# Pair 2 of the `up` product in seven half products, weight sums and sums of squares on GpSimd, and longer runs of feature matmuls, in a hybrid decoder layer on one core

## The chip, the cores and the metric

The kernel runs on one core of one Trainium2 chip. The metric is the time of one execution on the device, in microseconds (us). Three runs of the kernel before took 682.83 us in the median, from 681.87 to 683.28.

## The reference

One decoder layer over 512 tokens and 1024 features, all in float32. Two mixers (pooling over four windows, and sparse attention with 8 heads in 2 groups) are merged by gates and projected. A gated convolutional MLP follows. What the change touches is the two norms and the MLP's first product:

```
h = rms_norm(x, mix_norm_g)                 # mean of squares over 1024 features
proj = h @ w_in
...
x = x + (gate_pool * y_pool + gate_nsa * y_nsa) @ w_out
h = rms_norm(x, ffn_norm_g)
gate_pre, val = split(h @ w_up, 2)          # w_up: 1024 x 5632
gate_c = causal_dwconv(gate_pre, conv_w, conv_b)
x = x + (silu(gate_c) * val) @ w_down       # w_down: 2816 x 1024
```

## The kernel before

Everything is kept transposed: features on the 128 partitions, the 512 tokens along a row. A float32 product is made of three matmuls in a reduced format (`fp32r`): each operand is split into a high part and a low part (the rest), and high x high, high x low and low x high are added up in PSUM (`mm3`, line 479). So each weight tile `wraw` that a DMA brings is split into `whi` (ScalarE copies it into the reduced format) and `wlo` (VectorE subtracts, or ScalarE copies the negative and a DMA from GpSimd's queue adds the raw tile to it).

**Stages.** First the query and key projection with the sum of squares of the input (`square_x`, line 578; the sum goes through a matmul with ones, `norm_rstd`, line 588). Then attention, whose matmuls form the stream `m`, beside the feature products (gates, pooling, compression inputs), whose matmuls form the stream `f`; both share TensorE. Then the projections `wno` and `wout`, with the second sum of squares (line 1189). Then `up`: 22 pairs of 128 x 1024 weight blocks, one of the gate half and one of the value half. Products with `wdn` are filled in between pairs 5 and 18. Last the output stage with `wdz` (`dz_fast`, line 1419) in four pairs.

**Plain and fast pairs.** A plain pair (`up_plain`, line 1235) is two `mm3` over 8 blocks: 2 x 8 x 3 = 48 matmuls of 512 columns. A fast pair (`up_fast`, line 1343) takes the 2 x 2 block product with seven half products in the manner of Strassen: 7 x 4 x 3 = 84 matmuls of 256 columns (`product`, line 1261, with weights called a11, a12, h1 to h5). It needs sums of the weights (`half_weights`, line 1312): four additions of 128 x 512 tiles, s3 = first + r1, r1 = r1 + r2, rg = rg + r1, and the other half of rg plus the first; then each sum is split, some by a DMA from GpSimd's queue (`parts`, line 1320). `PLAIN = (0,2)` says that pairs 0 and 2 are plain. The output stage uses the same `half_weights` with tiles of 384 columns.

**Order.** The program is first recorded as a list of operations and then ordered by a planner (`Plan.run`, line 228, and `Plan.emit`, line 379): it prices each operation (`price`, line 199), plays the five engines' queues forward, and writes each engine's instructions in the order that it found. Each engine works through its own queue strictly in that order. On TensorE the planner picks between the heads of the streams `m` and `f` (line 301), by which has got less far.

All instructions are issued at line 422, so that in the profile the tile names tell them apart: `sl`, `sh` are the low and high part of a weight sum, `s`, `r`, `wraw` the sums and their sources, `th`, `tl`, `gh`, `gl`, `gp` parts of the normed input, `acc` and `sq` the sum of squares and one square, `mm`, `tr`, `av`, `sc` PSUM banks.

Of the kernel before, what the change touches and what calls it, by code (L numbers as in the profile page):

```python
# [49 lines left out]
NCST = _o  # L50
PAGES = 54
RINGS = {"wraw": 3, "whi": 3, "wlo": 3}
PLAIN = (0,2)
DIRECT = (0,)
AT = (5, 9, 13, 17)
FILL = {f: (0, 0, 0, 0) for f in range(22)}
# [1 line left out]
FILL.update({18: (0, 1, 0, 0), 19: (0, 0, 0, 0), 20: (0, 0, 0, 0), 21: (0, 0, 0, 0)})  # L58
TRIES = 12
RESERVE = 3  # L60
CUTS = (1, 2)
MORE = 4
BASE = 5.0
# [3 lines left out]
LANDS = (0.8, 0.8, 1.2, 1.2, 2.0, 2.0)  # L67
TRIALS = ((0.5, RATE), (0.8, RATE), (1.4, RATE), (0.8, 0.9 * RATE))
AHEAD = 4


def _span(x):
# [12 lines left out]
def _cols(x):  # L85
    n = 1
    for _, c in list(x.ap)[1:]:
        n *= c
    return n
# [23 lines left out]
class Plan:  # L113
# [45 lines left out]
    def note(self, eng, method, a, kw):  # L159
        if self.open is None or self.open == "new":  # L160
            op = Op(len(self.ops), eng, self.stream)
            op.deps.update(o.i for o in self.after)
            self.ops.append(op)
            if self.open == "new":
                self.open = op
        else:
            op = self.open
            assert op.eng == eng
        outs = [a[0]] if a else []
        outs += [v for k, v in kw.items() if k in self.OUT and v is not None]  # L170
        ins = [v for v in a[1:] if hasattr(v, "tensor")]
        ins += [v for k, v in kw.items() if k not in self.OUT and hasattr(v, "tensor")]
        op.calls.append((method, a, kw))
        cost, tail, land = self.price(eng, method, outs, ins, a, kw)
        op.cost += cost
        op.port |= eng == "POOL" and method[:6] == "tensor" or eng == "DVE" and not any(
            x.tensor.name in self.psum for x in ins)
        op.tail = tail
        op.land += land
        if kw.get("accum_op") is not None:  # L180
            ins.append(outs[0])
        for x, w in [(x, False) for x in ins] + [(x, True) for x in outs]:
            n = x.tensor.name
            if n not in self.tag:
                continue
            r = (0, 999, 0, 1 << 30) if n in self.psum and n not in self.fine else _span(x)
            past = list(self.writes.get(n, ()))
            if w:
                past += self.reads.get(n, ())
            for o, q in past:  # L190
                if o is not op and r[0] < q[1] and q[0] < r[1] and r[2] < q[3] and q[2] < r[3]:
                    op.deps.add(o.i)
            (self.writes if w else self.reads).setdefault(n, []).append((op, r))
            if not self.users[n]:
                op.allocs.append(n)
            if op not in self.users[n][-1:]:
                self.users[n].append(op)

    def price(self, eng, method, outs, ins, a, kw):
        n = max(_cols(x) for x in outs + ins)  # L200
        if method == "dma_start":
            x = outs[0]
            size = x.ap[0][1] * _cols(x) * 4 if hasattr(x, "ap") else 0
            return (0.87 if eng == "POOL" else 0.45), 0.0, size * (2.0 if kw.get("accum_op") is not None else 1.0)
        if eng == "PE":
            n = _cols(a[2])
            return max(n / 2250.0 + (0.005 if n < 300 else 0.0), 0.109), 0.17, 0
        if eng == "ACT":
            c = 0.19 + n * 0.000835
            if any(_cols(x) == 1 for x in ins):  # L210
                c += 0.09
            if kw.get("accum_out") is not None:
                c += 0.19
            if a[2] in (AF.Sin,):
                c += 1.28
            return c, 0.0, 0
        if eng == "DVE":
            wide = [x for x in ins if _cols(x) > 1]
            if method == "tensor_tensor_reduce":
                return 0.24 + n * 0.00105, 0.0, 0  # L220
            if len(wide) > 1 or method == "tensor_reduce" or any(x.tensor.name in self.psum for x in wide):
                return 0.15 + n * (0.00105 if method != "scalar_tensor_tensor" else 0.00114), 0.0, 0
            return 0.2 + n * 0.00054, 0.0, 0
        if method == "memset":
            return 0.1 + n * 0.0008, 0.0, 0
        return 0.12 + n * 0.0023, 0.0, 0

    def run(self, key, reserve, land, rate=RATE, fixed=None):
        ops = self.ops
# [17 lines left out]
        at = dict.fromkeys(heads, 0)  # L247
        done = {"m": 0.0, "f": 0.0}
        total = {s: sum(o.cost for o in l if s == "f" or self.span[0] <= o.i <= self.span[1]) for s, l in heads.items()}
        order = []  # L250

        def finish(o):
            for n in o.tiles:
# [42 lines left out]
        def pick(e):  # L296
            if fixed:
                o = fixed[e][count[e]] if count[e] < len(fixed[e]) else None
                w = None if o is None or o.left else when(o)
                return None if w is None else (w, o)  # L300
            if e == "PE":
                best = None
                for s, l in heads.items():
                    if at[s] < len(l) and not l[at[s]].left:
                        w = when(l[at[s]])
                        if w is not None:
                            first = (done["m"] <= min(done["f"] + self.lead, 0.999)) == (s == "m")
                            w2 = max(w - 0.1, clock[e]) if first else w + 1e-6
                            if best is None or w2 < best[0]:
                                best = (w2, w, l[at[s]])  # L310
                return best and (best[1], best[2])
            c = [(when(o), o) for o in pool[e]]
            c = [x for x in c if x[0] is not None]
            if not c:
                return None
            m = min(x[0] for x in c)
            return min(((key[o.i], w, o.i, o) for w, o in c if w <= m + 0.12))[1::2]

        dirty = dict.fromkeys(engs, True)
        while len(order) < len(ops):  # L320
            best = None
            for e in engs:
                p = pick(e)
                if p and (best is None or p[0] < best[0]):
                    best = p
            if settle(best[0] if best else 1e17):
                continue
            if best is None:
                raise RuntimeError("no order found: %d of %d" % (len(order), len(ops)))
            w, o = best  # L330
            o.start = w
            clock[o.eng] = w + o.cost
            if o.port:
                port[:] = [w + o.cost, o.eng]
            o.fin = w + o.cost + o.tail
            if o.land:
                queue[o.eng].append([w + o.cost + 0.7, o.land / rate, o])
            count[o.eng] += 1
            if o.eng == "PE":
                at[o.stream] += 1  # L340
                if o.stream == "f" or self.span[0] <= o.i <= self.span[1]:
                    done[o.stream] += o.cost / total[o.stream]
            else:
                pool[o.eng].remove(o)
            for n in o.allocs:
                g = self.tag[n]
                f = free[g]
                past = min(f)
                f.remove(past)
                for u in self.users.get(past[1], ()):  # L350
                    u.hand.append(o)
                if g in nxt:
                    nxt[g] += 1
                if n in self.early:
                    line[0] += 1
            order.append(o)
            if not o.land:
                finish(o)
# [67 lines left out]
def hybrid_layer(ctx: ExitStack, tc: tile.TileContext, xT, xa, pos, par, cst, poolw, w1, wa, wb, wf,  # L426
# [3 lines left out]
    PE, ACT, DVE, POOL, SP = pl.engines  # L430
# [98 lines left out]
    acc = page("acc")  # L529
# [48 lines left out]
    def square_x(k):  # L578
        if k == 0:
            ACT.activation(acc, xr[k], AF.Square)  # L580
        else:
            sq = page("sq")
            ACT.activation(sq, xr[k], AF.Square)
            DVE.tensor_add(acc, acc, sq)

    rb = keep("rb", (P, T))

# [137 lines left out]
    for t in range(NT):  # L725
        x, y = qp[t], kp[t]
# [182 lines left out]
    x = keep("kcx", (64, 1, DH))  # L909
    DVE.tensor_scalar_mul(x[:, 0], pk[0:64, 0:64], 0.5)  # L910
    sq = keep("kcs", (64, DH))
# [209 lines left out]
    for c in range(4):  # L1121
        wh, wl = weights(wno[c].rearrange("p a k n -> p (a k n)"), 1024, "v")
        for f in (2 * c, 2 * c + 1):
            o = (f % 2) * 512
# [3 lines left out]
            m = page("tn")  # L1128
# [16 lines left out]
    acc = page("acc")  # L1145
# [28 lines left out]
    for f in (0, 4, 1, 5, 2, 6, 3, 7):  # L1174
# [14 lines left out]
        if f:  # L1189
            sq = page("sq")  # L1190
            ACT.activation(sq, x2[f], AF.Square)
            DVE.tensor_add(acc, acc, sq)
        else:
            ACT.activation(acc, x2[f], AF.Square)
        if f > 3:
# [116 lines left out]
    def half_weights(first, second, w, dma, gate):  # L1312
# [16 lines left out]
        a1 = tuple(ring(n, F32R)[:, :2 * w] for n in ("whi", "wlo"))  # L1329
        split(*a1, rg)  # L1330
        s3 = soon("s3")[:, :w]
        DVE.tensor_add(s3, rg[:, :w], r1)
        h5 = parts(r2, dma[0])
        DVE.tensor_add(r1, r1, r2)
        h3 = parts(s3, dma[1])
        DVE.tensor_add(rg[:, :w], rg[:, :w], r1)
        h1 = parts(r1, dma[2])
        h2 = parts(rg[:, :w], dma[3])
        DVE.tensor_add(rg[:, w:], rg[:, w:], rg[:, :w])
        h4 = parts(rg[:, w:], dma[4])  # L1340
        return tuple(q[:, :w] for q in a1), tuple(q[:, w:] for q in a1), h1, h2, h3, h4, h5

# [106 lines left out]

    pl.emit(TRIES, RESERVE)  # L1450

# [93 lines left out]
```

## Time and profile before

| what | value |
|---|---|
| median of 3 runs | 682.83 us |
| the profiled execution's own time | 682.61 us |
| its span (first to last instruction) | 680.8 us |
| TensorE (PE) busy | 675.8 us, 99% |
| VectorE (DVE) busy | 529.2 us, 78% |
| ScalarE (ACT) busy | 446.5 us, 66% |
| GpSimd (POOL) busy | 106.9 us, 16% |
| mean granted TensorE clock | 0.999 |

A matmul's busy time overlaps the next one's, so what a matmul costs is read from the starts of two neighbours, or from a piece of the chain of waits with its count. In the chain each row is: start, duration, engine and what it wrote, and how many. In the timeline each row is: start, busy time, engine, operation, out<-in, shape, count, and in brackets idle time before it with what ended it. In the table by stretches of time, each engine's busy time stands with its instruction count behind it. GpSimd's rows named DMA are the time in which it issues the transfer; its spans are rough.

### The profile page before, as it was taken

What the parts mean: (1) busy time and instruction counts of PE and PEld (TensorE: products, weight loads), DVE (VectorE), ACT (ScalarE), POOL (GpSimd) and SP (SyncE); (2) the same over time, 40 slices, a digit from 0 to 9 for tenths busy, and PEclk for the clock granted to TensorE, in tenths of its full rate; (3) what the DMA queues carried; (4) which work ended last, traced back from release to release, by engine and by line L of the source; (5) the groups of instructions that cost most, each with busy time, mean ns of one, the idle gap of its engine ahead of it and who ended that gap; (6) DMA issues with size and microseconds to landing.
All of it is one profiled execution on the core that took longest, in us unless ns stands there. A gap on an engine that the chain in (4) does not pass through costs nothing.

```text
span 680.8 us, 11617 instructions
## 1 busy us (share of the span) xinstructions
PE 675.8 (99%) x4186; PEld 605.1 (89%) x4186; DVE 529.2 (78%) x1149; ACT 446.5 (66%) x821; POOL 106.9 (16%) x135
## 2 busy tenths in 40 slices
PE   9999999999999999999999999999999999999997
PEld 8898888888888888888898999999999999999897
DVE  6869777888877743868868988877777877888985
ACT  7677487777677653346777766667667665677552
POOL 0010111111100110001222222232212222222131
PEclk9999999999999999999999999999999999999999
DMA  8469656445455567845877778778859766775365
GB/s 303 146 160 273 156 133 161 109 125 143 120 143 136 127 150 245 286 152 171 232 167 194 167 164 189 187 172 197 188 127 191 199 156 168 177 164 129 70 145 154
DMA packets 49449, 115.34 MB, mean 169 GB/s; under 512 B 5616, under 2 KB 11632, under 8 KB 49392
## 3 DMA queue, kind: packets, MB, share of 16 engines
q1 hardware_dynamic: 31392, 76.44, 35.2%
q0 software_dynamic: 17856, 38.02, 31.2%
q8 instruction: 33, 0.54, 0.3%
q14 instruction: 24, 0.20, 0.1%
q10 hardware_dynamic: 144, 0.14, 0.1%
HBM read 70.28 MB, written 6.29 MB: 112 GB/s over the span
## 4 chain that ended last, share of the span: by engine, by line
PE 95%; DMA 2%; DVE 1%; ACT 0%; issue 0%; POOL 0%; SPq 0%; POOLq 0%; ACTq 0%
PE mm L422 37%; PE tr L422 33%; PE sc L422 14%; PE av L422 11%; DMA xr<-xT 1%; DMA sl<-wraw 1%; DMA r<-wdz 0%; DVE qp L422 0%; DVE small L422 0%; POOL sl L422 0%; SPq L422 0%; DVE vv L422 0%; ACT whi L422 0%; ACT xh L422 0%; ACT sl L422 0%
## 5 line engine op out<-in xcount | busy, mean ns | idle before, releaser
L422 ACT ACTIVATE whi<-wraw 128x1024 fp32r<-128x1024 f32 (+2 forms) x90 | 91.8, 1021 | 38.8 <-PE mm L422 13.2
L422 DVE TENSOR_TENSOR wlo<-wraw,whi 128x1024 fp32r<-128x1024 f32 (+1 forms) x62 | 72.4, 1169 | 4.6 <-ACT whi L422 4.2
L422 PE MATMUL mm<-xh,whi 128*128 128x512 f32 x176 | 71.3, 405 | 0.0
L422 PE MATMUL tr<-tl,sh 128*128 128x256 f32 x250 | 70.1, 280 | 0.0
L422 PE MATMUL mm<-xh,wlo 128*128 128x512 f32 x176 | 68.9, 391 | 0.0
L422 PE MATMUL mm<-xl,whi 128*128 128x512 f32 x176 | 68.7, 390 | 0.0
L422 PE MATMUL tr<-th,sl 128*128 128x256 f32 x240 | 67.7, 282 | 0.0
L422 PE MATMUL tr<-th,sh 128*128 128x256 f32 x240 | 67.7, 282 | 0.0
L422 POOL DMA_DIRECT2D wlo<-wraw x28 | 24.5, 877 | 240.3 <-ACT wlo L422 182.5
L422 POOL DMA_DIRECT2D sl<-r x44 | 38.0, 863 | 125.4 <-ACT sl L422 78.7
L422 PEld LDWEIGHTS tr<-tl,sh 128*128 128x128 f32 x250 | 47.2, 189 | 0.5
L422 PEld LDWEIGHTS tr<-th,sh 128*128 128x128 f32 x240 | 45.1, 188 | 1.1
L422 PEld LDWEIGHTS tr<-th,sl 128*128 128x128 f32 x240 | 45.1, 188 | 0.0
L422 ACT ACTIVATE u<-tr 128x256 f32<-128x256 f32 x40 | 15.4, 384 | 42.8 <-PE tr L422 42.3
L422 DVE SCALAR_TENSOR_TENSOR ft<-fg,pr,ft 128x511 f32<-128x511 f32 (+1 forms) x44 | 32.9, 748 | 12.0 <-ACT ft L422 11.5
L422 PE MATMUL sc<-yh,whi 128*128 128x512 f32 x108 | 42.2, 390 | 0.0
L422 PE MATMUL sc<-yl,whi 128*128 128x512 f32 x108 | 42.0, 389 | 0.0
L422 PE MATMUL sc<-yh,wlo 128*128 128x512 f32 x108 | 42.0, 389 | 0.0
L422 ACT ACTIVATE wlo<-wraw 128x1024 fp32r<-128x1024 f32 x28 | 29.7, 1061 | 16.0 <-PE mm L422 13.1
L422 PEld LDWEIGHTS mm<-xh,wlo 128*128 128x128 f32 x176 | 33.0, 188 | 7.3
L422 PEld LDWEIGHTS mm<-xh,whi 128*128 128x128 f32 x176 | 33.1, 188 | 5.6
L422 PEld LDWEIGHTS mm<-xl,whi 128*128 128x128 f32 x176 | 33.2, 188 | 5.5
(427 smaller groups left out, 2055.0 us busy)
## 6 DMA issues: line engine op xcount, KB each, us to landing
wlo<-wraw POOLq DMA_DIRECT2D x28, 512.0 KB, 4.7
wraw<-wup SPq DMA_DIRECT2D x24, 512.0 KB, 4.3
wraw<-wf SPq DMA_DIRECT2D x22, 512.0 KB, 3.6
r<-wup SPq DMA_DIRECT2D x40, 256.0 KB, 5.2
sl<-r POOLq DMA_DIRECT2D x40, 256.0 KB, 4.4
wraw<-wdn SPq DMA_DIRECT2D x16, 512.0 KB, 4.3
sl<-wraw POOLq DMA_DIRECT2D x20, 256.0 KB, 3.5
wraw<-wout SPq DMA_DIRECT2D x8, 512.0 KB, 3.6
```

The lines of the kernel that those rows point to most:

```text
L422: getattr(self.real[o.eng], method)(*a, **kw)
```

## The change

Four things change.

1. `PLAIN` loses pair 2, which so becomes a fast pair.
2. In `half_weights` two of the four additions (s3, and the last one into the second half of rg) move from VectorE to GpSimd, in the 21 fast pairs of `up` and the four of the output stage.
3. The 14 additions into `acc` of the two norms move from VectorE to GpSimd.
4. The planner keeps on with the stream `f` on TensorE, once it has begun it, until twelve matmuls in a row are placed, and prices GpSimd's two-input additions at 0.33 + 0.004 a column. It no longer marks operations that share a port; since nothing but DMAs and fills stood on GpSimd before, that mark had no effect there.

```
-PLAIN = (0,2)
+PLAIN = (0,)
...
+POOL2 = 0.004
...
+RUN = 12
...
-        op.port |= eng == "POOL" and method[:6] == "tensor" or eng == "DVE" and not any(
-            x.tensor.name in self.psum for x in ins)
...
-        return 0.12 + n * 0.0023, 0.0, 0
+        return 0.33 + n * (0.0026 if sum(_cols(x) > 1 for x in ins) < 2 else POOL2), 0.0, 0
...
                             first = (done["m"] <= min(done["f"] + self.lead, 0.999)) == (s == "m")
+                            if s == "f" and 0 < length[0] < RUN:
+                                first = True
+                            elif s == "m" and 0 < length[0] < RUN:
+                                first = False
...
+                length[0] = length[0] + len(o.calls) if o.stream == "f" else 0
...
             ACT.activation(sq, xr[k], AF.Square)
-            DVE.tensor_add(acc, acc, sq)
+            POOL.tensor_add(acc, acc, sq)
...
             ACT.activation(sq, x2[f], AF.Square)
-            DVE.tensor_add(acc, acc, sq)
+            POOL.tensor_add(acc, acc, sq)
...
         s3 = soon("s3")[:, :w]
-        DVE.tensor_add(s3, rg[:, :w], r1)
+        POOL.tensor_add(s3, rg[:, :w], r1)
...
-        DVE.tensor_add(rg[:, w:], rg[:, w:], rg[:, :w])
+        POOL.tensor_add(rg[:, w:], rg[:, w:], rg[:, :w])
         h4 = parts(rg[:, w:], dma[4])
```

What the planner makes of it is shown at three places. The first is GpSimd's queue while the second norm's squares are added up and the first fast pair's weights are made (`acc` is the sum of squares, `tl` and `gp` are parts of the normed input, `s`, `r` and `wraw` are weight sums). Before:

```order
L422 DMA tl<-tb 128x512
L422 DMA gp<-gh 128x256 x2
L422 DMA sl<-r_869 128x512
L422 DMA sl<-r_868 128x512
L422 DMA wlo<-wraw 128x1024
L422 DMA tl<-tb 128x512
L422 DMA wlo<-wraw 128x1024
L422 DMA sl<-wraw 128x512
```

And now:

```order
L427 DMA gp<-gh 128x256
L427 TENSOR_TENSOR acc<-acc,sq 128x512
L427 DMA gp<-gh 128x256
L427 DMA sl<-r_868 128x512
L427 DMA sl<-r_869 128x512
L427 TENSOR_TENSOR acc<-acc,sq 128x512
L427 DMA tl<-tb 128x512
L427 TENSOR_TENSOR wraw<-wraw 128x512
L427 DMA sl<-wraw 128x512
```

The last addition into `acc`, for which the norm waits, stands behind three DMA issues on this queue, and the last weight sum stands ahead of the issue that splits it; the two `wlo` transfers of the plain pair 2 are gone.

The second place is the end of GpSimd's queue: the last two pairs of the output stage. Before:

```order
L422 DMA sl<-r_1522 128x384
L422 DMA sl<-s_1525 128x384
L422 DMA sl<-wraw 128x384
L422 DMA sl<-r_1543 128x384
L422 DMA sl<-s_1546 128x384
L422 DMA sl<-wraw 128x384
```

And now:

```order
L427 DMA sl<-r_1534 128x384
L427 DMA sl<-s_1537 128x384
L427 TENSOR_TENSOR wraw<-wraw 128x384
L427 DMA sl<-wraw 128x384
L427 TENSOR_TENSOR s_1558<-wraw,r_1554 128x384
L427 DMA sl<-r_1555 128x384
L427 DMA sl<-s_1558 128x384
L427 TENSOR_TENSOR wraw<-wraw 128x384
L427 DMA sl<-wraw 128x384
```

Where three issues followed one another, two additions now stand between them, the second just ahead of the last issue of the program.

The third place is TensorE late in attention (`mm` rows are the stream `f`, `av` rows the stream `m`). Before:

```order
L422 MATMUL mm<-xh,wlo 128x512
L422 MATMUL av<-pt,vv 128x512
L422 MATMUL mm<-xh,whi 128x512
L422 MATMUL mm<-xl,whi 128x512
L422 MATMUL mm<-xh,wlo 128x512
L422 MATMUL av<-pt,vv 64x512
L422 MATMUL av<-pt,vv 128x384
L422 MATMUL mm<-xh,whi 128x512
```

And now:

```order
L427 MATMUL mm<-xh,wlo 128x512
L427 MATMUL av<-pt,vv 128x512
L427 MATMUL av<-pt,vv 64x512
L427 MATMUL av<-pt,vv 128x384
L427 MATMUL av<-pt,vv 64x384
L427 MATMUL av<-pz,vv 128x256
L427 MATMUL av<-pz,vv 64x256
L427 MATMUL av<-pz,vv 128x256
L427 MATMUL av<-pz,vv 64x256
L427 MATMUL mm<-xh,whi 128x512
```

Where three feature matmuls stood between single matmuls of attention, the attention's eight stand together, with at least twelve feature matmuls on either side. Between the first transposes of attention and the first `wno` matmul, TensorE's order had 82 runs of feature matmuls before, 38 of them of three matmuls, and has 45 now, none under twelve; with the attention's pieces between them that is 164 pieces before and 90 now.

More of the change, by code (lines that the diff above doesn't have):

```diff
@@ L249, in run @@
         total = {s: sum(o.cost for o in l if s == "f" or self.span[0] <= o.i <= self.span[1]) for s, l in heads.items()}
-        order = []
+        order, length = [], [0]
         def finish(o):
```

## Prediction

> **What bounds the kernel now.** I read the page first, then TensorE's waits, the chain, and then, stage by stage, how early the other engines are.
>
> ```profile
> span 680.8 us, 11617 instructions
> PE 675.8 (99%) x4186; PEld 605.1 (89%) x4186; DVE 529.2 (78%) x1149; ACT 446.5 (66%) x821; POOL 106.9 (16%) x135
> PE 95%; DMA 2%; DVE 1%; ACT 0%; issue 0%; POOL 0%; SPq 0%; POOLq 0%; ACTq 0%
> ```
>
> TensorE is busy all through the span and makes up 95% of the chain. A busy TensorE could still hide waits, so its waits come next.
>
> ```profile
> PE mm L422 <- POOL ones L422: 1.0, 1, 1.0
> PE tr L422 <- ACT whi L422: 0.3, 1, 0.3
> PE tr L422 <- DMA sl<-wraw: 0.2, 1, 0.2
> ```
>
> These are all its waits: 1.0 us at the start, 0.3 in the first stage, 0.2 at the end. So a gain can only come from less work or closer packing on TensorE, and relief for VectorE is worth nothing by itself; a loss comes wherever another engine gets late. The sum is made on the profiled execution, 682.61 us, 0.22 us under the median of the runs. About 0.2% (1.4 us) is what a measurement of this kernel can tell from no change.
>
> **Pair 2.** Two rows of the chain, both inside `up`, give TensorE's price by width:
>
> ```profile
> 363.03 5.44 PE av L422 x24
> 379.82 4.25 PE tr L422 x36
> ```
>
> The first is one plain product of 512 columns, 5.44 / 24 = 0.2267 us a matmul; the second is half products, 4.25 / 36 = 0.118. The plain pair costs 48 x 0.2267 = 10.88 us, the fast one 84 x 0.118 = 9.92. The change takes off 0.96 us. Half products are a little dearer per column, so the saving is 9%, not an eighth. This stands on the path whole, if the seven weights are ready.
>
> They are ready if the lead that other fast pairs have holds. For h4, whose low part is made last, the issue on GpSimd and the first matmul are shown for the first and the last of the 20 fast pairs:
>
> ```profile
> 353.65 0.86 POOL L422 DMA_DIRECT2D sl<-wraw  x1 [0.91 <-ACT sl L422]
> 372.57 0.40 PE L422 MATMUL mm<-gh,sh 128*128 128x256 f32 x2
> 617.83 0.86 POOL L422 DMA_DIRECT2D sl<-wraw  x1 [2.18 <-DVE sl L422]
> 634.69 0.40 PE L422 MATMUL tr<-gh,sh 128*128 128x256 f32 x2
> sl<-wraw POOLq DMA_DIRECT2D x20, 256.0 KB, 3.5
> ```
>
> That is 18.9 and 16.9 us from issue to use; less the 3.5 us to landing, over 13 us are left. Pair 2 now needs such weights itself, one pair after pair 1, in a stretch where VectorE loses ten additions. I cost its preparation at nothing; this lead hides it. If the cover were gone, TensorE would wait for it by what a fast pair's preparation takes longer than its 9.92 us; VectorE's share of a fast pair is 8.6 us (worked out below), so even then it keeps up.
>
> **Runs of twelve.** What a change of kind costs on TensorE is read from starts around two groups of transposes between feature matmuls:
>
> ```profile
> 143.55 0.93 PE L422 MATMUL tr<-cs,pp 128*128 128x128 f32 x7
> 144.23 0.47 PE L422 MATMUL mm<-xh,whi 128*128 128x512 f32 x1
> 144.55 0.39 PE L422 MATMUL mm<-xl,whi 128*128 128x512 f32 x1
> 146.40 0.49 PE L422 MATMUL tr<-cs,pp 128*128 128x128 f32 x3
> 146.96 0.39 PE L422 MATMUL mm<-xl,whi 128*128 128x512 f32 x1
> ```
>
> Seven transposes and a matmul take 144.55 - 143.55 = 1.00 us, three and a matmul 0.56. Four transposes are thus 0.44, and 1.00 - 0.77 - 0.227 leaves 0.00 for the change there and back, with an error of some 0.02 from rounded starts. So a change of kind costs between 0 and 0.02 us; I take the middle, 0.01. Of 164 pieces 90 are left, 74 changes fewer: 0.7 us off, between 0 and 1.5. Attention's matmuls wait longer for their turn, by at most one run of twelve, 12 x 0.2267 = 2.7 us, and their softmax gains the same 2.7 us of cover; pieces of attention without cover grow no longer than some already there, so I cost new waits here at nothing.
>
> **The additions on GpSimd.** No row shows an addition on GpSimd. The nearest are VectorE's own additions of that size, and GpSimd's fills:
>
> ```profile
> L422 DVE TENSOR_TENSOR s<-wraw,r 128x512 f32<-128x512 f32 x11 | 7.5, 682 | 0.0
> L422 DVE TENSOR_TENSOR wraw<-wraw 128x512 f32<-128x512 f32 x10 | 6.9, 689 | 0.2
> 68.19 0.86 POOL L422 MEMSET kcz<- 128x512 f32 x1
> 68.66 0.86 POOL L422 MEMSET cst<- 128x512 f32 x1
> ```
>
> The fills start 0.47 us apart: one pass over 512 columns. An addition reads two tiles and writes one. My estimate, three passes, is 1.4 us. The ends are 0.47 (one pass) and five passes, 2.4 us, about what the changed planner itself assumes (0.33 + 512 x 0.004 = 2.38). The GPSIMD Engine Reference of the Trainium skill, in "Elementwise — side-by-side cycle accounting", gives 4497 ns for 2048 columns; a quarter is an estimate of 1.1 us, which no run here shows and which would leave the sum as it is. VectorE loses 2 x 0.69 = 1.37 us in each fast pair, which nothing waits for. Ahead of GpSimd's split issues now stand two additions a pair, 2.8 us (at most 4.8): they and those behind them use up that much of the 13 us. Nothing on the path.
>
> At the first norm:
>
> ```profile
> 15.82 3.07 DVE L422 TENSOR_TENSOR acc<-acc,sq 128x512 f32<-128x512 f32 x4
> 30.55 0.95 PE L422 MATMUL mm<-ones,acc 128*128 128x1 f32 x8
> ```
>
> The sum is ready at 18.9 and wanted at 30.6. Seven additions on GpSimd, from about 10 us, end at 20 (27 at 2.4 each). Nothing. The second norm is tighter:
>
> ```profile
> 341.25 0.69 DVE L422 TENSOR_TENSOR acc<-acc,sq 128x512 f32<-128x512 f32 x1
> 343.48 0.95 PE L422 MATMUL sc<-ones,acc 128*128 128x1 f32 x8
> 347.93 1.13 DVE L422 SCALAR_TENSOR_TENSOR diag<-cs,rstd,diag 128x128 fp32r<-128x128 f32 x4
> 349.19 0.62 PE L422 MATMUL tr<-diag,ones 128*128 128x512 f32 x2
> ```
>
> The addition has from 341.25 to 343.48, 2.2 us; at 1.4 it fits, at 2.4 it is 0.2 late. I take nothing. While this addition waits for its square, the `tl` issue and the first fast pair's last weight sum wait behind it on GpSimd; both are for products that have the lead above. Behind it the chain to the diagonal ends at 349.06 for a matmul at 349.19: no cover there, which matters to a rival below.
>
> The end has no lead either:
>
> ```profile
> 662.46 3.31 DMA r<-wdz
> 666.70 0.55 DVE L422 TENSOR_TENSOR s<-wraw,r 128x384 f32<-128x384 f32 x1
> 668.35 0.56 DVE L422 TENSOR_TENSOR wraw<-wraw,r 128x384 f32<-128x384 f32 x1
> 666.90 0.86 POOL L422 DMA_DIRECT2D sl<-r  x1 [5.21 <-ACT sh L422]
> 670.36 0.86 POOL L422 DMA_DIRECT2D sl<-wraw  x1 [1.39 <-ACT sl L422]
> 670.36 4.89 DMA sl<-wraw
> ```
>
> The last weights land at 665.8. Then s3 (384 columns, 1.05 us) ends at 666.9 on a GpSimd that is idle, where VectorE had ended at 667.25; two issues of 0.86 fill GpSimd to 668.6; the last sum, whose source VectorE has ready at 668.4 as it is relieved of one addition, runs to 669.7; ScalarE's copy (0.5) leads to an issue at 670.2, against 670.36 before. So at 1.4 us nothing changes. At 2.4 (1.8 for 384) both additions stretch and the issue moves to about 671.7, 1.3 us late. SyncE's queue now has the last loads behind three output transfers, where a fourth stood before: they may go out up to one half product, 9 x 0.118 = 1.06 us, earlier. I take zero.
>
> Sum: 682.61 - 0.96 - 0.7 = 680.95, so 681.0.
>
> **The rivals.**
>
> *Late additions* eat most of the gain. If an addition takes 2.4 us, the end is 1.3 us late and the second norm 0.2, with up to 1.06 back: 680.95 + 1.3 = 682.3, within 0.2%. For it speak the missing leads at both places; against it, 1.4 us from the fills.
>
> *GpSimd and VectorE block each other*, and it is slower. What the trace has is VectorE beside fills and DMA issues, which do not read tiles. It keeps its 0.69 us beside the second fill:
>
> ```profile
> 68.75 0.69 DVE L422 TENSOR_TENSOR kcb<-kc,pr 128x512 f32<-128x512 f32 x1
> ```
>
> If VectorE's two-input operations stand still while GpSimd adds, its load counts:
>
> ```profile
> 461.50:553.80 92.30, 92.30 (x650) 86.64 (x649) 70.50 (x116) 61.34 (x106) 22.41 (x26) 1.00 0.76 180
> 600.00:620.00 20.00, 20.00 (x171) 20.00 (x171) 17.36 (x32) 15.41 (x28) 4.31 (x5) 1.00 0.61 134
> ```
>
> In the first stretch six pairs of 15.38 us hold 70.5 / 6 = 11.75 us of VectorE: less 1.37, plus 4.8 blocked at the worst, 15.2, still inside. In the second, two pairs of 9.92 hold 17.36, 8.6 each (the stretch is 0.16 longer than the pairs): less 1.37 plus twice the addition. It reaches 9.92 at 1.35 us an addition. At 2.4 it is 12.0, 2.1 over, in the last four pairs (results go straight into the output stage) 8.4 us, and the second norm's chain loses one addition, 2.4: 682.61 - 1.7 + 10.8 = 691.7. At 1.8 it is 4 x 0.9 + 1.8 = 5.4: 686.3. At 1.4 only the norm's 1.4 is left: 682.3. The Trainium skill states this as a rule (SBUF — State Buffer, "Who interferes with whom"): a VectorE instruction with two SBUF inputs contends with a GpSimd instruction that reads SBUF, and the later one blocks. By that rule the time is one of the three just given; no run here shows it yet.
>
> *More is gained*: 0.02 us a change of kind (1.5), and the last loads early enough to take away the 0.2 us wait: 682.61 - 0.96 - 1.5 - 0.2 = 679.95.
>
> That pair 2 stays as it was is excluded: TensorE's order holds its 84 half-width matmuls.
>
> **How the numbers follow.** Forecast 680.95: 0.46. More gained: 0.10. Late additions: 0.28. Blocking: 0.16, of which 0.02 light, within 0.2%. Faster 0.46 + 0.10 = 0.56, same 0.28 + 0.02 = 0.30, slower 0.14. The range goes from 679.7 (679.95, less the noise of the runs) to 684.5; above lie the heavier blocking cases, below almost nothing, together under 0.2.
>
> **What would show it.** Right: TensorE's waits stay under 1.5 us in all, matmuls of 256 columns rise by 84 and those of 512 fall by 48, an addition on GpSimd takes 1 to 2 us, VectorE's additions keep 0.69 us, and attention's stretch is 0.5 to 1 us shorter. Wrong: a wait of TensorE on `acc`, on `diag` or on `sl` of over 1 us; VectorE's two-input operations stretched where GpSimd adds; waits within attention for a softmax that comes too late.

## The result, and the profile after

The changed kernel took 691.09 us in the median of 5 runs (689.86 to 692.92), the kernel before 682.83 (681.87 to 683.28): a ratio of 1.0122 (1.011 to 1.0133). It is 8.3 us slower, where 681.0 was forecast, and outside the range. The profiled execution took 692.92 us, the longest of the five. From its page, and all of TensorE's waits from 0.4 us on:

```profile
span 690.8 us, 11799 instructions
...
PE 679.8 (98%) x4222; PEld 610.0 (88%) x4222; DVE 532.3 (77%) x1096; ACT 447.5 (65%) x829; POOL 197.7 (29%) x200
...
PE 88%; DVE 6%; ACT 3%; issue 2%; DMA 1%; SPq 0%; DVEq 0%; ACTq 0%
```

```profile
PE tr L427 <- DVE wlo L427: 3.6, 1, 3.6
PE tr L427 <- ACT diag L427: 1.2, 1, 1.2
PE mm L427 <- POOL ones L427: 1.0, 1, 1.0
PE tr L427 <- ACT u L427: 0.8, 1, 0.8
PE av L427 <- ACT av L427: 0.4, 1, 0.4
PE av L427 <- ACT u L427: 0.4, 1, 0.4
```

TensorE's share of the chain fell from 95% to 88%, and waits on VectorE and ScalarE have come. The second thing to see is VectorE: it no longer makes the 64 additions (56 of 512 columns at 0.69 us and 8 of 384 at 0.55, some 43 us of work), and is busy for 532.3 us where it was 529.2.

Four marks on TensorE, taken from the trace in every kernel of this study, show where the time goes: the first transposes of attention, the second norm's diagonal, the first product with `wdn` and the last matmul.

| kernel | attention | diagonal | first `wdn` | last |
|---|---|---|---|---|
| before | 52.60 | 349.19 | 391.00 | 677.17 |
| after | 59.91 | 357.68 | 401.30 | 687.24 |
| lost up to here | 7.3 | 8.5 | 10.3 | 10.1 |

So 7.3 us go before attention starts, 1.7 more up to the diagonal (and 0.5 had been won in between), 1.8 in the first pairs of `up`, where pair 2 was to save 0.96; after that 0.2 is won.

**First place, the first projection.** VectorE's groups from 10.2 to 24.5 us, before and then after (count | busy us, mean ns | idle):

```profile
L422 DVE TENSOR_TENSOR wlo<-wraw,whi 128x768 fp32r<-128x768 f32 x6 | 5.6, 954 | 0.6 <-ACT whi L422 0.5
L422 DVE TENSOR_TENSOR acc<-acc,sq 128x512 f32<-128x512 f32 x7 | 4.8, 690 | 0.4
L422 DVE SCALAR_TENSOR_TENSOR xl<-xr,x,xh 128x512 fp32r<-128x512 f32 x6 | 4.4, 746 | 0.0
```

```profile
L427 DVE SCALAR_TENSOR_TENSOR xl<-xr,x,xh 128x512 fp32r<-128x512 f32 x5 | 6.5, 1316 | 0.2 <-ACT xh L427 0.2
L427 DVE TENSOR_TENSOR wlo<-wraw,whi 128x768 fp32r<-128x768 f32 x3 | 4.0, 1321 | 0.5 <-ACT whi L427 0.5
L427 DVE TENSOR_SCALAR ang<-ang 128x40 f32<-128x40 f32 x3 | 2.5, 830 | 0.1
L427 DVE CAST posf<-ps_i 128x5 f32<-128x5 int32 x1 | 1.3, 1261 | 0.0
```

The seven additions are gone from VectorE, and what is left takes nearly twice as long; a cast of 5 columns takes 1.26 us. What stands beside it on GpSimd, and TensorE's wait, both in the changed kernel's timeline:

```profile
10.94 1.55 POOL L427 TENSOR_TENSOR acc<-acc,sq 128x512 f32<-128x512 f32 x1 [10.00 <-ACT sq L427]
12.88 9.51 POOL L427 TENSOR_TENSOR acc<-acc,sq 128x512 f32<-128x512 f32 x6 [0.39 <-ACT sq L427]
```

```profile
25.49 1.65 PE L427 MATMUL tr<-wlo,xh 128*128 128x512 f32 x3 [3.61 <-DVE wlo L427]
```

TensorE's clock in this stretch (the number after POOL's busy time in the stretches), before and then after:

```profile
25.00:30.00 5.00, 5.00 (x29) 4.34 (x29) 4.38 (x20) 4.81 (x9) 0.00 (x0) 1.00 0.49 143
```

```profile
20.00:25.00 5.00, 1.88 (x13) 1.50 (x11) 4.83 (x10) 1.89 (x2) 2.31 (x2) 0.91 0.00 0
25.00:30.00 5.00, 4.51 (x13) 3.74 (x14) 4.79 (x18) 1.09 (x3) 0.00 (x0) 0.50 0.63 200
30.00:35.00 5.00, 5.00 (x29) 4.48 (x28) 2.11 (x4) 3.43 (x7) 0.00 (x0) 0.90 0.36 118
```

After the wait the clock is at half: 13 matmuls in five microseconds instead of 29. Of the 7.3 us, 3.6 are the wait itself; TensorE then works for 5.5 us, from 25.5 to 31.0, at half clock, which by this count loses half of that, some 2.7 us.

**Second place, the second norm.** VectorE before, and then VectorE, GpSimd and TensorE in the changed kernel:

```profile
344.66 0.17 DVE L422 CAST nrv<-nrv 128x4 f32<-128x4 int32 x1
```

```profile
352.45 1.89 DVE L427 CAST nrv<-nrv 128x4 f32<-128x4 int32 x1
...
352.71 1.59 POOL L427 TENSOR_TENSOR wraw<-wraw 128x512 f32<-128x512 f32 x1
...
357.68 0.89 PE L427 MATMUL tr<-diag,ones 128*128 128x512 f32 x2 [1.19 <-ACT diag L427]
```

A cast of 4 columns in the chain to the diagonal, 0.17 us before, ends when the first fast pair's weight sum on GpSimd ends. This chain had no cover.

**Third place, the first pairs of `up`.** The same in pair 2's stretch, again first the row of before (the mean of this operation from 350 to 640 us):

```profile
L422 DVE SCALAR_TENSOR_TENSOR ft<-fg,pr,ft 128x510 f32<-128x510 f32 x22 | 16.4, 748 | 0.5
```

```profile
376.34 2.50 DVE L427 SCALAR_TENSOR_TENSOR ft<-fg,pr,ft 128x510 f32<-128x510 f32 x1
...
376.68 1.59 POOL L427 TENSOR_TENSOR s<-wraw,r 128x512 f32<-128x512 f32 x1
```

0.75 became 2.50 us. The chain of waits runs through `ft` for 18% of the stretch from 366 to 392 us. In the whole trace 41 of VectorE's operations on SBUF tiles that lie beside an addition take over 0.1 us longer than the median of the same operation alone, 37.9 us longer together; of the 42 with an operand in PSUM none does. 37 of the 41 begin after the addition has begun, so there the later one waits; the other four are recorded as beginning 0.26 to 0.44 us ahead of it, the cast and the `ft` above among them, and why these wait the trace does not show. Two groups from 350 to 640 us, the second before and after, show the difference:

```profile
L427 DVE TENSOR_TENSOR x<-sc,x 128x512 f32<-128x512 f32 x27 | 18.6, 689 | 12.1 <-PE sc L427 12.1
...
L422 DVE TENSOR_TENSOR yl<-y,yh 128x512 fp32r<-128x512 f32 x20 | 13.7, 685 | 0.5 <-ACT yh L422 0.4
...
L427 DVE TENSOR_TENSOR yl<-y,yh 128x512 fp32r<-128x512 f32 x20 | 17.6, 879 | 0.0
```

`x` reads a PSUM bank and keeps its 0.69 us; `yl` had 0.685 before. GpSimd seems to wait in its turn: after idle time, with nothing of the kind beside it, an addition of 512 columns takes 1.27 to 1.29 us, and beside a `wlo` of 1024 columns that began 0.6 us earlier 1.73 to 1.80. Not all of the difference between the additions is waiting: eight that stand directly behind other work of GpSimd take 1.58 to 1.61 us with no VectorE operation on SBUF tiles alone beside them.

```profile
L427 POOL TENSOR_TENSOR s<-wraw,r 128x512 f32<-128x512 f32 x21 | 32.4, 1541 | 4.2 <-DMA r<-wup 2.3 <-PE tr L427 1.3 <-issue 0.5
...
L427 POOL TENSOR_TENSOR acc<-acc,sq 128x512 f32<-128x512 f32 x14 | 23.0, 1640 | 17.2 <-ACT sq L427 16.8
```

### The profile page after: what moved, and what is told of

Its sections match the earlier page's. It is cut to its first block, busy times and chain, and to the rows that moved or that the text cites. A ratio compares the mean times of both kernels' runs of the same rounds, so it can differ in the third digit from the quotient of the medians.

```text
span 690.8 us, 11799 instructions
## 1 busy us (share of the span) xinstructions
PE 679.8 (98%) x4222; PEld 610.0 (88%) x4222; DVE 532.3 (77%) x1096; ACT 447.5 (65%) x829; POOL 197.7 (29%) x200
## 4 chain that ended last, share of the span: by engine, by line
PE 88%; DVE 6%; ACT 3%; issue 2%; DMA 1%; SPq 0%; DVEq 0%; ACTq 0%
PE mm L427 35%; PE tr L427 28%; PE sc L427 14%; PE av L427 12%; DVE ft L427 1%; DMA xr<-xT 1%; ACT whi L427 1%; DVE gh L427 1%; DVE sl L427 1%; DVE xl L427 0%; DVE ang L427 0%; DVE nrv L427 0%; DVE wlo L427 0%; ACT sl L427 0%; ACT sh L427 0%
## 5 line engine op out<-in xcount | busy, mean ns | idle before, releaser
L427 DVE TENSOR_TENSOR wlo<-wraw,whi 128x1024 fp32r<-128x1024 f32 (+1 forms) x63 | 74.8, 1188 | 8.0 <-ACT whi L427 5.9
L427 POOL TENSOR_TENSOR wraw<-wraw 128x512 f32<-128x512 f32 (+1 forms) x25 | 35.3, 1414 | 93.1 <-issue 36.1
L427 POOL DMA_DIRECT2D sl<-r x46 | 42.7, 935 | 37.5 <-ACT sl L427 13.3
L427 DVE SCALAR_TENSOR_TENSOR ft<-fg,pr,ft 128x511 f32<-128x511 f32 (+1 forms) x44 | 37.1, 842 | 7.7 <-ACT ft L427 7.0
L427 ACT ACTIVATE pp<-pp,asm 128x384 f32<-128x384 f32 (+3 forms) x64 | 35.4, 555 | 8.6 <-DVE asm L427 8.5
L427 POOL TENSOR_TENSOR s<-wraw,r 128x512 f32<-128x512 f32 (+1 forms) x25 | 36.7, 1468 | 14.1 <-DMA wraw<-wdz 7.4
L427 ACT ACTIVATE sl<-r 128x512 fp32r<-128x512 f32 (+1 forms) x46 | 28.1, 612 | 9.9 <-DMA r<-wdz 4.1
L427 PE MATMUL tr<-tl,sh 128*128 128x256 f32 x121 | 33.9, 281 | 0.0
L427 ACT ACTIVATE sh<-wraw 128x512 fp32r<-128x512 f32 (+1 forms) x50 | 30.2, 603 | 3.8 <-DVE wraw L427 3.8
L427 PE MATMUL tr<-th,sh 128*128 128x256 f32 x110 | 31.1, 283 | 0.8 <-ACT u L427 0.8
```

What stands on the lines that cost most here:

```text
L427: getattr(self.real[o.eng], method)(*a, **kw)
```

## The experiments

Theory A: GpSimd's additions and VectorE's operations on SBUF tiles shut each other out, and the held operations make TensorE late. Theory B: the order is bad, since the planner made a new one, in which for instance the position angles (`ang`) stand ahead of `xl` and `wlo` on VectorE. All ratios are to the kernel before, run on the same chip; medians that are compared below come from different chips, on which the kernel before took 682.59 to 682.83 us.

### The order kept, the additions moved

Here the planner's order stays and only the engine is changed on which an addition is issued:

```
-    marks = ()
+    marks, moved = (), {}
...
-                getattr(self.real[o.eng], method)(*a, **kw)
+                getattr(self.real[self.moved.get(o.i, o.eng)], method)(*a, **kw)
...
             POOL.tensor_add(acc, acc, sq)
+            pl.moved[pl.last().i] = "DVE"
...
         POOL.tensor_add(s3, rg[:, :w], r1)
+        pl.moved[pl.last().i] = "DVE"
...
         POOL.tensor_add(rg[:, w:], rg[:, w:], rg[:, :w])
+        pl.moved[pl.last().i] = "DVE"
```

**All 64 of the changed kernel back on VectorE.**

> The changed kernel with its order of every engine kept, only the 64 adds that it gave to GpSimd are issued on VectorE at the same place in the order. Theory A (GpSimd's two-input add and VectorE's operations between SBUF tiles shut each other out): the loss goes, the SCALAR_TENSOR_TENSOR xl in the first product takes 0.75 us again instead of 1.5 to 1.8, the first transposes of attention come at 52 to 54 us as before (59.91 in the changed kernel), and the time is 681 to 684 us. Theory B (the planner's new order is itself bad: it puts the position angles ahead of two xl and two wlo on VectorE): the first transposes still come after 57 us and the time stays at 687 to 691 us.

682.17 us, ratio 1.0 (0.9986 to 1.0014). From its page, TensorE's waits and the timeline:

```profile
span 679.7 us, 11732 instructions
...
PE 674.7 (99%) x4222; PEld 607.3 (89%) x4222; DVE 532.0 (78%) x1160; ACT 447.3 (66%) x829; POOL 107.7 (16%) x136
```

```profile
PE mm L427 <- POOL ones L427: 1.0, 1, 1.0
PE av L427 <- ACT u L427: 0.4, 1, 0.4
PE tr L427 <- ACT tr L427: 0.3, 1, 0.3
```

```profile
52.18 1.03 PE L427 MATMUL tr<-cs,qp 128*128 128x128 f32 x8
```

The same order without GpSimd's additions is 8.9 us faster (8.3 by the ratios). Theory A holds and B falls for this order: the angles ahead of `wlo` do no harm by themselves. VectorE is busy for 532.0 us with the 64 additions and 532.3 without them: being held used up the relief.

**Only the first norm's seven back on VectorE (the `pl.moved` line in `square_x` alone); then only the 50 weight sums back (the two such lines in `half_weights` alone).**

> The changed kernel with its order kept, only the seven adds of squares of the first norm are issued on VectorE, the other 57 stay on GpSimd. If the losses of the three places stand by themselves (7.3 us before attention, 1.7 at the second norm, about 2 in the first pairs of up), the first transposes of attention come at 52 to 53 us and the time is 683.5 to 684.5 us. If the places are coupled (VectorE late in one is late in the next), it is below 683 or above 686 us.

> The changed kernel with its order kept, only the 50 weight sums of the fast pairs are issued on VectorE, the 14 adds of squares stay on GpSimd. If the losses stand by themselves, the first norm's 7.3 us stay and what the second norm and up lose goes, but for the adds of squares beside VectorE: 688 to 690 us. The cast of the second norm's chain (1.89 us beside a weight sum) takes below 0.3 us again.

685.81 us, 1.0046 (1.003 to 1.0063), and 687.64 us, 1.0073 (1.0053 to 1.0093). Over the 682.17 us of the first experiment, the 57 additions without the first norm cost 3.6 us, the two norms' 14 cost 5.5; together 9.1, and all 64 cost 8.9 (by the ratios 3.1, 5.0 and 8.3). The second norm's seven are in both, so that the two parts add up says that these seven cost next to nothing. The first norm alone is the larger part. In the first of these the cast at the second norm takes 1.89 us again, in the second 0.28, and there the diagonal loses nothing after attention: that 1.7 us is the weight sum's, not the sums of squares'. The first norm costs 5.3 us in the medians (691.09 - 685.81) and more in the profile, since the profiled execution of the changed kernel spent more time at half clock than the other four (0.994 in the mean, against 0.998).

**The weight sums on GpSimd from the seventh fast pair on, all else on VectorE.** As in the first experiment, but in `half_weights`, behind both sums:

```
+    early = []
...
+        if len(early) < 12:
+            early.append(1)
+            pl.moved[pl.last().i] = "DVE"
```

> The changed kernel with its order kept; all sums of squares and the two weight sums of the first six fast pairs are issued on VectorE, the weight sums of the other pairs (38 adds) on GpSimd. If an add costs only where VectorE's results have no lead, these 38 cost nothing: 681.5 to 683 us, with VectorE's operations held beside them for over 10 us in all. If every add costs by what it holds, 684 us and more. Either way VectorE's relief is worth nothing, so it is not below the 682.17 us of the same order with all adds on VectorE.

681.79 us, 0.9989 (0.9979 to 0.9998). The first of the two groups of additions on GpSimd, and then `yl` on VectorE from 350 to 640 us:

```profile
L427 POOL TENSOR_TENSOR s<-wraw,r 128x512 f32<-128x512 f32 x15 | 23.1, 1538 | 2.9 <-DMA r<-wup 2.9
```

```profile
L427 DVE TENSOR_TENSOR yl<-y,yh 128x512 fp32r<-128x512 f32 x20 | 17.6, 880 | 0.0
```

`yl` is held as long as in the changed kernel (880 ns), and 38 additions cost nothing, the last four pairs and the output stage among them. Being held costs only where the result has no lead. Here some relief is left, 521.4 us busy against 532.0 with all 64 on VectorE, of some 25 us that the 38 additions take there; it gains nothing.

**In the order of before: the first norm's seven on GpSimd; then all 62.** The kernel before, with the issuing line changed as above, and the line below behind the first norm's addition, or behind every such addition:

```
             DVE.tensor_add(acc, acc, sq)
+            pl.moved[pl.last().i] = "POOL"
```

> The kernel before with its order of every engine kept, only the seven adds of squares in the first norm are issued on GpSimd. Theory A (shut out): VectorE's xl and wlo between 10 and 23 us take 1.5 to 2.1 us where they lie beside an add, TensorE waits for wlo or xl for over 1.5 us before 30 us, and the time is 685 to 691 us. Theory B (order): nothing but seven adds changes, VectorE has 4.8 us less to do there, and the time is 682 to 683 us.

> The kernel before with its order kept, all sums of squares and both weight sums of each fast pair issued on GpSimd. Theory A alone (each add costs where it falls): as in the changed kernel the second norm and the first pairs of up lose 2 to 5 us, 685 to 688 us. Theory C (an add costs only where the order leaves VectorE's results no lead; the order of before leaves it): 683 to 684.5 us, and VectorE's operations beside adds are stretched all the same.

683.17 us, 1.0011 (1.0002 to 1.002), and 690.79 us, 1.0117 (1.0102 to 1.0132). VectorE from 10.2 to 24.5 us in the first of the two:

```profile
L422 DVE TENSOR_TENSOR wlo<-wraw,whi 128x768 fp32r<-128x768 f32 x5 | 8.1, 1643 | 1.3 <-ACT whi L422 1.3
L422 DVE SCALAR_TENSOR_TENSOR xl<-xr,x,xh 128x512 fp32r<-128x512 f32 x5 | 6.7, 1366 | 0.0
```

They are held just as in the changed kernel, but attention starts at 52.62: in this order `wlo` stands ahead of the angles and has lead enough, so what I expected of theory A there was wrong. With all 62 the loss is as large as the changed kernel's and lies elsewhere: the diagonal comes 3.1 us late, the first `wdn` product 6.5, the end 8.1. Not all of this is VectorE being held. TensorE here waits for GpSimd's sum of squares itself, and 1.1 us at the end (0.2 before) for the DMA behind the last weight sum, which are the late additions of the prediction's first rival:

```profile
PE sc L422 <- POOL acc L422: 1.2, 1, 1.2
```

The second part of theory C falls: the order of before has lead at the first norm only. So the order decides where additions on GpSimd cost, and neither order has room for them at the second norm and in the first pairs.

### What holds VectorE

The kernel before, with a copy on GpSimd issued right behind each of the first norm's additions on VectorE:

```
-    marks = ()
+    marks, extra = (), {}
...
+            for e, method, a in self.extra.get(o.i, ()):
+                getattr(self.real[e], method)(*a)
...
             DVE.tensor_add(acc, acc, sq)
+            pl.extra[pl.last().i] = [("POOL", "tensor_copy", (rb, sq))]
```

> The kernel before with its order kept and its seven adds of the first norm on VectorE; beside each, GpSimd copies the same square into a tile that is not yet in use (one input where the add has two). If GpSimd holds VectorE by any operation on SBUF, xl and wlo between 10 and 23 us are stretched to 1.3 us and more as beside the adds. If two inputs are what holds it, xl takes 0.75 us and wlo 0.96 us.

One execution took 683.4 us, too few to say anything of the time. VectorE from 10.2 to 24.5 us:

```profile
L422 DVE TENSOR_TENSOR acc<-acc,sq 128x512 f32<-128x512 f32 x7 | 6.1, 873 | 0.4
L422 DVE SCALAR_TENSOR_TENSOR xl<-xr,x,xh 128x512 fp32r<-128x512 f32 x6 | 4.7, 802 | 0.0
L422 DVE TENSOR_TENSOR wlo<-wraw,whi 128x768 fp32r<-128x768 f32 x4 | 3.7, 947 | 0.0
```

Neither expectation holds clean. Copies stand beside few `xl` and `wlo`, but beside most of the additions, which take 0.873 instead of 0.69 us: a copy holds VectorE too, less (the copy takes 0.67 us alone, the addition 1.27). The fill shown in the prediction held nothing. This is the rule that the blocking rival cited (the Trainium skill, SBUF — State Buffer, "Who interferes with whom"): two SBUF inputs on VectorE against a GpSimd instruction that reads SBUF, and casts and `tensor_scalar` too in their two-port modes. The traces agree: operations with two SBUF inputs were held, and so were the casts (the one of 4 columns for 1.89 us) and the `tensor_scalar` on `ang` (0.83 us in the mean); which mode these last ran in, no trace shows.

### Planned anew

**The changed kernel with the sums of squares on VectorE (the first line pair below, in both norms); with all additions on VectorE (all three pairs); with the planner's rule and its old price put back (the last part).**

```
-            POOL.tensor_add(acc, acc, sq)
+            DVE.tensor_add(acc, acc, sq)
...
-        POOL.tensor_add(s3, rg[:, :w], r1)
+        DVE.tensor_add(s3, rg[:, :w], r1)
...
-        POOL.tensor_add(rg[:, w:], rg[:, w:], rg[:, :w])
+        DVE.tensor_add(rg[:, w:], rg[:, w:], rg[:, :w])
```

```
+        op.port |= eng == "POOL" and method[:6] == "tensor" or eng == "DVE" and not any(
+            x.tensor.name in self.psum for x in ins)
...
-        return 0.33 + n * (0.0026 if sum(_cols(x) > 1 for x in ins) < 2 else POOL2), 0.0, 0
+        return 0.12 + n * 0.0023, 0.0, 0
```

> The changed kernel with both sums of squares back on VectorE (planned anew), the two weight sums of each pair left on GpSimd. If the two norms carry the loss as the profile of the changed kernel has it (7.29 us up to attention, 1.71 up to the second norm's diagonal) 681 to 683 us are left: what is over the kernel before then comes from the first pairs of up (TensorE's gaps of 0.59, 0.96 and 0.61 us at 377 to 391 us). If the weight sums carry it, 687 us and more.

> The changed kernel with all 64 adds on VectorE (planned anew): pair 2 by half products and runs of twelve alone. My sum of the prediction for these two, -0.96 and -0.7 us, gives 681.0 to 681.5 us, TensorE's waits below 2 us. If the first fast pairs cannot be prepared in time without the relief of VectorE (pair 2 is one more of them in a row), TensorE waits over 1 us between 360 and 400 us, and the time is 682.5 to 685 us.

> The changed kernel with the planner's rule that the diff deletes put back (an add on GpSimd and an operation of VectorE without an operand in PSUM don't overlap in the plan) and its old price of an add, 1.30 us, near the 1.27 us that the changed kernel's trace shows where nothing is beside it. If the order is bad because the planner no longer knows that the two shut each other out, the waits of TensorE go below 3 us and the time is 681 to 685 us. If no order has room for 64 adds of 1.3 us, it stays at 688 us or more.

684.64 us, 1.0032 (1.0022 to 1.0043); 687.04 us, 1.0066 (1.0045 to 1.0087); 693.83 us, 1.0165 (1.0145 to 1.0185). The second is the surprise. It has the same instructions on the same engines as the first experiment of all, and is 4.9 us slower: TensorE waits for ScalarE's evictions `u` (2.4 us) and in the output stage. Here the order does decide. And a planner that marks the exclusion and prices an addition at 1.30 us instead of 2.38 found no better order with the additions on GpSimd. TensorE waits for `acc` at the second norm and for a `wlo` in the first projection:

```profile
PE sc L429 <- POOL acc L429: 4.1, 1, 4.1
PE tr L429 <- DVE wlo L429: 2.5, 1, 2.5
```

**Pair 2 alone** (the kernel before with the first edit); **runs of twelve alone** (the changed kernel with all additions on VectorE, as above, and the second).

```
-PLAIN = (0,2)
+PLAIN = (0,)
```

```
-PLAIN = (0,)
+PLAIN = (0,2)
```

> The kernel before with pair 2 of up by seven half products, planned anew; no GpSimd adds, no runs of twelve. My term for it is -0.96 us with the preparation hidden: 681.5 to 682.0 us. In the changed kernel's order with its adds on VectorE, the second fast pair waits 0.59 us for an eviction at 367.69; if such waits belong to the extra fast pair, they take the 0.96 us back, and the time is 682.3 us or more.

> The kernel before with runs of twelve feature matmuls alone, planned anew. My term is -0.7 us within attention; the two orders with runs of twelve run so far gave -0.53 us there (from the first transposes to the first wno product less what was moved over its edges). If that is all it changes, 681.8 to 682.3 us. If runs of twelve also let TensorE reach the first products of up or the end with less prepared, TensorE waits more behind 340 us and the time is 683 us or more.

689.33 us, 1.0098 (1.0067 to 1.0129), and 682.39 us, 0.9999 (0.9989 to 1.0008). Pair 2 alone waits in several pairs; here one, in ScalarE's and then TensorE's timeline:

```profile
449.69 0.63 ACT L422 ACTIVATE sl<-r 128x512 fp32r<-128x512 f32 x1 [3.37 <-DMA r<-wup]
...
454.20 0.36 ACT L422 ACTIVATE u<-av 128x256 f32<-128x256 f32 x1
```

```profile
454.62 0.39 PE L422 MATMUL av<-th,sh 128*128 128x256 f32 x1 [1.67 <-ACT u L422]
```

A split of a later pair's weights waits 3.37 us for its load at the head of ScalarE's queue, and the eviction `u` that TensorE needs stands behind it.

**The same instructions in other orders.** Only a number of the planner is changed: it assumes slower transfers (in pair 2 alone, and in the changed kernel with all additions on VectorE), or a later base for its due times (in pair 2 alone).

```
-RATE = 331000.0
+RATE = 290000.0
```

```
-BASE = 5.0
+BASE = 7.0
```

> Pair 2 alone as before, only the planner assumes transfers 12% slower (290 instead of 331 KB per us); every instruction is the same. If the order is what loses, leaving too little between a load's landing and the queue that waits for it, the waits at 390, 452 and 672 us change and the time is 682 to 686 us. If one more fast pair is too much work for VectorE and ScalarE, it stays at 687 us or more.

> Pair 2 alone, only the planner's base for due times is 7 instead of 5 us, which gives another order of the same instructions. If the order decides, the time is another one, by over 1.5 us either way from the 689.33 us of the first order of pair 2. If the work decides, it is within 1.5 us of it.

> Pair 2 and runs of twelve with all adds on VectorE (687.04 us as first planned), only the planner assumes transfers 12% slower. If the order decides, 681 to 685 us; my two terms for these edits would give 681.0 us if it had no new waits. If the work decides, 686 us or more.

Pair 2 with slower transfers assumed: 681.56 us, 0.999 (0.9978 to 1.0001). With the later base: 687.95 us, 1.0089 (1.006 to 1.0117), within the 1.5 us that I had set against the order. Pair 2 and runs of twelve with slower transfers assumed: 682.94 us, 1.0004 (0.9991 to 1.0016). So the two orders with slower transfers assumed are 7.8 and 4.1 us faster than the first ones of the same instructions. All of TensorE's waits in the first of them:

```profile
PE mm L422 <- POOL ones L422: 1.0, 1, 1.0
```

**The whole change, and pair 2 alone again, with slower transfers assumed.**

> The whole change with the planner's transfers 12% slower (290 instead of 331 KB per us), all 64 adds on GpSimd. If the loss of the changed kernel is that of one unlucky order, 682 to 685 us. If the adds on GpSimd lose in any order of a planner that doesn't know what they hold, 687 us or more, with waits of TensorE before 30 us, at the second norm or in the first pairs of up.

> Pair 2 by half products alone in the order planned with slower transfers, in five rounds. My term for pair 2 is -0.96 us, and its first profile showed -0.95 between the second norm and the output products: 681.3 to 681.9 us, a ratio of 0.998 to 0.999 whose interval ends below 1.

694.12 us, 1.0167 (1.0151 to 1.0182): with the additions on GpSimd the order so planned loses too, 11.2 us over the 682.94 with all of them on VectorE. And 681.33 us, 0.9985 (0.9976 to 0.9994): pair 2 alone in this order is the fastest version here, 1 to 1.4 us faster than before; the changed kernel is beaten by 9.8 us.

## Why the prediction was wrong, point by point

- **The step that failed** is "The additions on GpSimd", where I wrote for the first norm "The sum is ready at 18.9 and wanted at 30.6. … Nothing." I priced when the sum would be late. The sum was in time; what was late were VectorE's other operations, which the additions held: TensorE waited 3.6 us for a `wlo`, and its clock halved. All 64 cost 8.9 us in the changed kernel's order.
- **The rival was named and placed wrong.** *GpSimd and VectorE block each other* had 0.16 and 691.7 us at its worst. The mechanism is what happened; that the number lies near 691.09 is chance. It is the case of an addition of 2.4 us; at 1.4 us, which is nearer to what was measured, I had 682.3 (and left out 0.4 us that my own limit of 1.35 us leaves over in four pairs). I had 8.4 us of the worst case in the last four pairs, since I counted VectorE's load per pair, and nothing at the first norm. The pairs lost nothing: being held meets a lead there. At the second norm I had 2.4 us for a held chain; it lost 1.7.
- **The addition's duration** was right: 1.4 us estimated, 1.27 at the shortest, 1.45 to 1.64 in the means of the three groups of 512 columns.
- **"Relief for VectorE is worth nothing by itself"** held, and more: with all 64 moved there was no relief, 532.3 us busy against 532.0.
- **Pair 2**: the term was right, its "preparation at nothing" was not. In the order without new waits (pair 2 alone, slower transfers assumed) the diagonal to the first `wdn` product is 0.95 us shorter, against 0.96 forecast. But I had looked at the lead of h4 alone. In the first order of pair 2 alone, which cost 6.7 us, a split that waits for a late load stands ahead of an eviction in ScalarE's queue.
- **Runs of twelve**: mis-sized. Attention from its first transposes to the first `wno` product took 220.17 us before and 219.63 in the changed order, 0.53 less instead of 0.7; its feature pieces fell from 82 to 45. But pair 2 alone with slower transfers has 85 pieces and is as short, 219.59. So no price of a change of kind shows, which is the lower end that I gave, and the 0.5 comes of something else in the order; what, stays open. Alone, runs of twelve can't be told from no change.
- **The end** lost nothing in the changed kernel, as forecast. In the order of before it lost 1.6 us after the first `wdn` product, with a wait of 1.1 us for the last `sl`.

What stays open is why the planner's own comparison does not see the waits that tell its orders apart. The late load is shown at one place and argued for the others.

## What to carry to other kernels

Before work is moved from VectorE to GpSimd, look at what VectorE does beside it, and not only at when the moved result is wanted: with all 64 additions moved, VectorE stood still for 37.9 of the 43 us that it was relieved of. It costs where a held result has no lead, so keep such work away from first stages, norm chains and first pairs. And where a planner sets the order, compare the edit with its order kept: two orders of the same instructions lay 4 to 8 us apart, where pair 2 itself is worth 0.95.

## What the runs showed of the hardware that I had not expected

- A held operation's length does not count: a cast of 4 columns was held for 1.89 us by an addition of 512.
- A wait of 3.6 us on TensorE halved its clock (0.50 from 25 to 30 us), as did the 4.1 us wait of the kernel with the planner's rule put back (0.52 from 350 to 355 us); in that same run the wait of 2.5 us did not:

```profile
25.00:30.00 5.00, 5.00 (x29) 4.29 (x29) 3.99 (x18) 3.57 (x5) 0.00 (x0) 1.00 0.63 218
...
350.00:355.00 5.00, 4.99 (x16) 4.32 (x17) 2.97 (x8) 1.15 (x2) 3.35 (x3) 0.52 0.43 75
```

The Trainium skill (TensorE: Matmul & The Clock Gate, "HAM oscillation — how this bites in real kernels") says to leave TensorE no gaps above some 3.4 us. These three waits agree with it, and the two long ones cost some 2.7 and 3.4 us more, half of the time that TensorE then worked at half clock.

- Shorter waits close together can do it too. In the order of before with all 62 on GpSimd no wait of TensorE was over 1.5 us, and yet its clock was at half from 354.2 to 357.6 us, behind a wait of 1.44 and one of 0.44 us with a single matmul between them:

```profile
352.27 0.50 PE L422 MATMUL tr<-diag,ones 128*128 128x512 f32 x1 [1.44 <-ACT diag L422]
...
355.00:356.00 1.00, 1.00 (x6) 1.00 (x6) 0.67 (x2) 1.00 (x2) 0.07 (x1) 0.50 0.94 344
```

Here the measurement goes beyond that sentence: a bound on single gaps is not enough. Waits of 2.2 and 2.5 us elsewhere in these runs left the clock whole, so what decides between them stays open.
